# Moving three things in a two-layer attention kernel on one core: the load of the norms' factors, one weight block, and the splitting of the next layer's memory

## The chip, the core and the metric

The kernel runs on one core of a Trainium2 chip. The engines are TensorE (PE: matrix products and transposes), ScalarE (ACT), VectorE (DVE) and GpSimd (POOL); SyncE (SP) only issues transfers. The metric is the time of one execution in device microseconds (us); the median of several runs is given, and one execution is also recorded by the hardware profiler.

## The reference

Two layers transform `x` (256 x 1024) with a memory `mem` (256 x 1024). In each layer 16 heads of 64 attend: six over a causal block, six in a dilated pattern, four over the memory. Everything is float32.

```python
def hybrid_layer(x, mem, norm_g, w_in, w_out, mem_norm_g, w_mem_kv, qk_g):
    h = rms_norm(x, norm_g)
    proj = jnp.einsum('btd,de->bte', h, w_in)
    ...
    a_q, a_k, a_v, a_g, b_q, b_k, b_v, b_g, m_q, m_g = jnp.split(proj, cuts, axis=-1)
    qa = rope(rms_norm(to_heads(a_q, N_HEADS_MOBA), qk_g[0]))
    ...
    oa = from_heads(moba_attention(qa, ka, to_heads(a_v, N_HEADS_MOBA)))
    ...
    ob = from_heads(dilated_attention(qb, kb, to_heads(b_v, N_HEADS_DIL)))
    mkv = jnp.einsum('bmd,de->bme', rms_norm(mem, mem_norm_g), w_mem_kv)
    m_k, m_v = jnp.split(mkv, 2, axis=-1)
    ...
    om = from_heads(memory_attention(qm, km, to_heads(m_v, N_HEADS_MEM)))
    y = jnp.concatenate([oa * jax.nn.silu(a_g), ob * jax.nn.silu(b_g), om * jax.nn.silu(m_g)], axis=-1)
    return x + jnp.einsum('bte,ed->btd', y, w_out)

def reference(x, mem, norm_g, w_in, w_out, mem_norm_g, w_mem_kv, qk_g):
    for layer in range(DEPTH):
        x = hybrid_layer(x, mem, norm_g[layer], w_in[layer], w_out[layer],
                         mem_norm_g[layer], w_mem_kv[layer], qk_g[layer])
    return x
```

With 256 rows the causal heads have a single block, so they attend causally within it; the three dilated patterns become one mask with logarithms of counts.

## The kernel before

**Split products.** A float32 product is made of three faster ones: each operand is split into a rounded part and a rest. Of a weight tile (`raw`) ACT makes `hi` with a cast (L430) and DVE the rest `lo` (L431). Of the activations, transposed so that the 1024 inner elements lie in eight blocks of 128 partitions, ACT makes `xmh`, scaled by the norm's factors (L183), and DVE `xml` (L186), both in `split_x`, two blocks at a time. PE runs hi·xmh, hi·xml and lo·xmh into `acc` (L111). PE also transposes by a product with `ident` (L114).

**The factors.** `gT` (128 x 32, 16 KB) holds the factors of both layers' norms of `x` and of `mem`, one column to a block. It is loaded at the start from POOL (L85), whose transfers go by a software queue. The memory of each layer is `memT`, the transposed memory, times its columns of `gT`; in layer 0 the first two blocks are not split but scaled whole (`whole`, L494), and multiplied with `raw` in full float32.

**Loads.** `load_mem` (L99) loads pieces of `memT` through SP; `loads` (L409) issues the weights unit by unit. The first unit (`raw0`, four blocks of 256 KB of the first layer's `w_mem_kv`) goes through ACT's queue, everything after through SP's, in the order of the code at L450 to L465. The weights of w_in follow as buffers (three) come free.

**Order of the work.** PE's instructions are kept in the order of the code (`pe`). Beside that, generators are spawned with a delay on a modelled clock; `poll` runs those that are due at each step of a projection. So `pair_of_heads` and `head` (scores `wk`<-`qkT`, the negated maximum `nm` L332, exponentials `pr` L334, their scaling L347, the transposes of `pr`, the copy `pT` L358, the products `o`) are woven between the projections of the next heads. `next_mem` is such a generator, too: it splits the next layer's memory, two blocks (two `xmh`, two `xml`) each time it is resumed, four times, with D_NEXT_MEM of the model's clock between.

**A layer** projects memory keys and values, `mq`, `mg`; then for kind 2 (the dilated side, the second one in the weights: `bq`, `bk`, `bv`, `bg`) and then kind 0 (the causal side, the first one: `aq` to `ag`) it runs `project`, `normed`, `start_heads`, `gates`; then the output products. `normed` needs the head's sums of squares `hss` (L263), `ms`, a power on POOL (`hrs`, L156), and tables `tab` of rotation times factors that POOL builds after the memory's heads are started (L204 to L209: four `tab` operations for each of the kinds 0 to 3, in this order, and one scaling ahead of kind 0 and of kind 2). `t` (L267) is the first instruction to read the part of the table of kind 2. What runs between two kinds is set by `poll`, and the order on ACT, DVE and POOL is then laid down by a scheduler where `pin` doesn't hold it.

Of the kernel before, what the change touches and what calls it, by code (L numbers as in the profile page):

```python
# [22 lines left out]
DEPTH = 2  # L23
# [43 lines left out]
def hybrid_kernel(ctx: ExitStack, tc: tile.TileContext, x, mem, mem_t, gains, w_in, w_out, w_mem_kv, qk_g, const, out):  # L67
    nc = tc.nc
# [13 lines left out]
    mhalf = cp.tile([P, 16], F32, name="mhalf")  # L82
    nc.vector.memset(mhalf, -0.5)
    gT = cp.tile([P, 32], F32, name="gT")
    tc.keep_in_program_order(nc.gpsimd.dma_start(gT, gains))  # L85
    ident = cp.tile([P, P], F32, name="ident")
    make_identity(nc, ident)
    pinning = [True]
# [1 line left out]
    def pin(ins):  # L90

        return tc.keep_in_program_order(ins) if pinning[0] else ins
# [5 lines left out]
    def load_mem(k0, k1):  # L98
        pin(nc.sync.dma_start(memT[:, k0:k1], mem_t[k0 * P:k1 * P, :].rearrange("(k p) t -> p k t", p=P)))  # L99
# [34 lines left out]
    def spawn(gen, delay):  # L134
        tasks.append([clock[0] + delay, gen])
# [30 lines left out]
    def xm_tiles():  # L166
        return [sp.tile([P, KD, T], F32R, tag=c, name=c, bufs=2) for c in ("xmh", "xml")]
# [48 lines left out]
    def project(xs, chunk, n):  # L216

        accs = [acc_p.tile([P, 512], F32, tag="acc", name="acc")[:, :n] for _ in range(NT)]

        def steps():  # L220
            for k0, nk, w in chunk:
                if len(w) == 1:
                    for k in range(nk):
                        for t in range(NT):
                            mm(accs[t], whole[k0 + k][:, t * P:(t + 1) * P], w[0][:, k], start=k0 + k == 0, stop=False)
                        yield
                    continue
                for ks in [range(nk)] if pinning[0] and nk < 4 else [[k] for k in range(nk)]:
                    products([(accs[t], k0 + k, [x[:, k0 + k, t * P:(t + 1) * P] for x in xs], [p[:, k] for p in w])
                              for t in range(NT) for k in ks], 0, KD - 1)  # L230
                    yield

        return accs, steps()

    def project_t(xs, chunk, n):

        accs = [acc_p.tile([P, 512], F32, tag="acc", name="acc")[:, :T] for _ in range(n // P)]

        def steps():
            for k0, nk, w in chunk:  # L240
                for k in range(nk):
                    products([(acc, k0 + k, [x[:, k0 + k] for x in xs], [p[:, k, e * P:(e + 1) * P] for p in w])
                              for e, acc in enumerate(accs)], 0, KD - 1, x_moves=True)
                    yield

        return accs, steps()

    def run(projection):
        accs, steps = projection
        for _ in steps:  # L250
            poll()
        return accs
# [4 lines left out]
    def normed(acc, n, dst, tables):  # L257

        h = n // HD
        sq = sp.tile([P, n], F32, tag="sq", name="sq", bufs=2)  # L260
        pin(nc.scalar.activation(sq, acc, AF.Square))
        ss = sp.tile([P, h], F32, tag="hss", name="hss", bufs=4)
        pin(nc.vector.tensor_reduce(ss, heads(sq), axis=AX.X, op=ALU.add))  # L263
        rs = sp.tile([P, h], F32, tag="hrs", name="hrs", bufs=4)
        rsqrt(rs, ss, h, 1.0 / HD)
        t1 = sp.tile([P, n], F32, tag="t1", name="t1", bufs=2)
        pin(nc.vector.tensor_tensor(heads(t1), heads(acc), tables[0][:, None, :].to_broadcast([P, h, HD]),  # L267
                                    op=ALU.mult))
        if len(tables) > 1:
            t2 = sq  # L270
            half = dict(s=2, d=HD // 2)
            pin(nc.vector.tensor_tensor(t2.rearrange("p (h s d) -> p h s d", **half),
                                        acc.rearrange("p (h s d) -> p h s d", **half)[:, :, ::-1, :],
                                        tables[1].rearrange("p (s d) -> p s d", s=2)[:, None]
                                        .to_broadcast([P, h, 2, HD // 2]), op=ALU.mult))
            pin(nc.vector.tensor_tensor(t1, t1, t2, op=ALU.add))
        pin(nc.vector.tensor_tensor(heads(dst), heads(t1), rs.unsqueeze(2).to_broadcast([P, h, HD]), op=ALU.mult))
# [111 lines left out]
    def loads():  # L389
        while loaded[0] < len(units):  # L390
            u = loaded[0]
            loaded[0] += 1
            i, a, nk, n = units[u]
            l, c = order[i]
            if c == "mkv":
                src = w_mem_kv[l]
            elif c in in_cols:
                src = w_in[l][:, in_cols[c][0]:in_cols[c][0] + n]
            else:
                src = w_out[l][e_rows[c][0] * P:, :]  # L400
            if u == 0:
                raws[u] = sp.tile([P, nk, n], F32, tag="yT0", name="raw0", bufs=1)
            else:
                raws[u] = wp.tile([P, nk, n], F32, tag="raw", name="raw", bufs=RAW_BUFS)
            step = 1 if u == 0 else 2 if u == 1 else 4 if u == 2 else nk
            for b in range(0, nk, step):
                e = b + step
                queue = nc.scalar if u == 0 else nc.sync
                pin(queue.dma_start(raws[u][:, b:e],  # L409
                                    src[(a + b) * P:(a + e) * P, :].rearrange("(k p) n -> p k n", p=P)))  # L410
                yield
# [24 lines left out]
    def weights():  # L436

        i = at[0]
        at[0] += 1
        while at[1] < len(splits) and units[splits[at[1]][0]][0] == i:  # L440
            s = at[1]
            at[1] += 1
            split(s + ahead[0])
            yield splits[s][1], splits[s][2], parts[s]
# [5 lines left out]
    for k in range(4):  # L450
        next(loading)
        if k < 2:
            load_mem(k, k + 1)
        elif k == 2:
            load_mem(2, 4)
    pin(nc.scalar.activation(cp.tile([P, 16], F32, name="table"), mhalf, AF.Square))
    load_mem(4, 6)
    next(loading)
# [13 lines left out]
    def next_mem(dst, g):  # L472

        for k2 in range(0, KD, 2):
            pinning[0] = True
            split_x(dst, memT[:, k2:k2 + 2], g, k2)
            pinning[0] = False
            yield D_NEXT_MEM

    for l in range(DEPTH):  # L480
# [47 lines left out]
        def gates(accs, dst):  # L528
            for e, acc in enumerate(accs):
                th = sp.tile([P, T], F32, tag="th", name="th", bufs=2)  # L530
                nc.scalar.activation(th, acc, AF.Tanh, scale=0.5)
                nc.vector.scalar_tensor_tensor(dst[:, e], th, 1.0, acc, op0=ALU.add, op1=ALU.mult)

        def head_tiles(n, nv):
            return [sp.tile([P, NT, n], F32, tag=c, name=c, bufs=1) for c in ("qn", "kn")] + [
                sp.tile([P, NT, nv], F32, tag="v", name="v", bufs=2),
                sp.tile([P, n // P, T], F32, tag="gate", name="gate", bufs=2)]
# [8 lines left out]
        def start_heads(pairs, e0, qn, kn, masks, v, gate, ready, delay=D_NORM):  # L546
            for pair in range(pairs):
                spawn(pair_of_heads(qn, kn, pair, masks, v, gate, ready,
                                    lambda y, e=e0 + pair: finished(y, e)), delay + D_PAIR * pair)
# [30 lines left out]
        for kind, e0 in ((2, 3), (0, 0)):  # L580
            if kind == 2:
                masks = [cst[:, C_DIL:C_DIL + 128], cst[:, C_DIL + 128:C_DIL + 384]]
            else:
                masks = [cst[:, C_CAUSAL + 128:C_CAUSAL + 256], cst[:, C_CAUSAL:C_CAUSAL + 256]]
            if l + 1 < DEPTH and kind == 2:
                mem_xs = xm_tiles()
                spawn(next_mem(mem_xs, gT[:, 24 + 8 * l:32 + 8 * l]), D_FIRST_MEM)
            qn, kn, v, gate = head_tiles(384, 384)
            ready = dict(v=1e9, gate=1e9)
            for i, dst in ((0, qn), (1, kn)):  # L590
                for t, acc in enumerate(run(project(xs, weights(), 384))):
                    normed(acc, 384, dst[:, t], (tab[:, kind + i, 0, t], tab[:, kind + i, 1, t]))
            start_heads(3, e0, qn, kn, masks, v, gate, ready)
            for t, acc in enumerate(run(project(xs, weights(), 384))):
                nc.scalar.copy(v[:, t], acc)
            ready["v"] = clock[0] + D_EVAC
            gates(run(project_t(xs, weights(), 256)), gate[:, 0:2])
            gates(run(project_t(xs, weights(), 128)), gate[:, 2:3])
            ready["gate"] = clock[0] + D_EVAC
# [64 lines left out]
```

## Time and profile before

| what | value |
|---|---|
| runs, median (lowest to highest) | 296.41 us (295.67 to 296.65), 3 runs |
| profiled execution | 295.58 us |
| its span | 293.8 us |
| PE busy | 285.1 us, 97% |
| DVE busy | 204.5 us, 70% |
| ACT busy | 200.1 us, 68% |
| POOL busy | 56.0 us, 19% |
| HBM read | 45.96 MB, 160 GB/s over the span |

The span runs from the first to the last recorded instruction; the time of the execution is 1.8 us longer. An engine that is busy for a small share may still hold up PE for a moment; these moments are found in the waits and timelines, not in this table.

### The profile page before, as it was taken

How to read it: one execution, taken by the hardware profiler on the slowest of the kernel's cores; microseconds unless marked ns; L12 is line 12 of the kernel's file. 1: busy time of each engine (PE TensorE's matmuls, PEld its weight loads, DVE VectorE, ACT ScalarE, POOL GpSimd, SP SyncE). 2: the span in 40 equal slices, each digit the busy share in tenths (PEclk: the TensorE clock that was granted, in tenths of full speed). 3: DMA queues.
4: the chain of work that ended last, by engine and by line, in shares of the span. 5: the costliest groups of instructions: out<-in, count | busy, mean ns of one | idle time of the engine just before them, and what ended most of it. 6: DMA issues, size and time to landing. Idle time of an engine off the chain costs nothing.

```text
span 293.8 us, 4977 instructions
## 1 busy us (share of the span) xinstructions
PE 285.1 (97%) x1810; PEld 250.2 (85%) x1810; DVE 204.5 (70%) x456; ACT 200.1 (68%) x445; POOL 56.0 (19%) x74
## 2 busy tenths in 40 slices
PE   7799999999999999999999999999999999999994
PEld 5489989698998999877788999989899899987773
DVE  1588899887656997654485668879655699765413
ACT  2799968795888646987364654868588864698600
POOL 1003598030001230000011049703000123000000
PEclk9999999999999999999999999999999999999999
DMA  7999656327347248246207726560823715820003
GB/s 231 378 366 355 208 143 229 78 102 220 106 113 240 62 158 310 98 166 207 80 8 243 222 101 174 189 172 9 274 60 108 240 47 170 304 99 29 3 0 143
DMA packets 32681, 47.33 MB, mean 161 GB/s; under 512 B 1152, under 2 KB 27536, under 8 KB 32656
## 3 DMA queue, kind: packets, MB, share of 16 engines
q1 hardware_dynamic: 32048, 45.95, 48.4%
q10 hardware_dynamic: 576, 1.05, 1.0%
q8 instruction: 14, 0.23, 0.3%
q14 instruction: 11, 0.09, 0.1%
q0 software_dynamic: 32, 0.02, 0.0%
HBM read 45.96 MB, written 1.05 MB: 160 GB/s over the span
## 4 chain that ended last, share of the span: by engine, by line
PE 81%; DVE 6%; DMA 5%; ACT 3%; issue 2%; POOL 1%; SPq 0%; DVEq 0%; ACTq 0%
PE acc L111 64%; PE wk L114 7%; PE o L111 5%; PE wk L111 5%; DMA raw<-in_w_in_dram 3%; DMA memT<-in_mem_t_dram 2%; DVE lo L431 2%; DVE xml L186 1%; ACT hi L430 1%; POOL hrs L156 1%; DVE hss L263 1%; ACT xmh L183 1%; POOL r L156 0%; DVE ms L155 0%; ACT pr L334 0%
## 5 line engine op out<-in xcount | busy, mean ns | idle before, releaser
L431 DVE TENSOR_TENSOR lo<-raw,hi 128x768 fp32r<-128x768 f32 (+1 forms) x91 | 97.2, 1091 | 31.0 <-ACT hi L430 30.9
L430 ACT CAST hi<-raw 128x768 fp32r<-128x768 f32 (+1 forms) x91 | 83.8, 937 | 33.0 <-PE acc L111 24.4
L111 PE MATMUL acc<-hi,xmh 128*128 128x384 f32 (+2 forms) x252 | 67.0, 348 | 1.7 <-ACT hi L430 1.7
L111 PE MATMUL acc<-hi,xml 128*128 128x384 f32 (+2 forms) x252 | 63.6, 335 | 0.0
L111 PE MATMUL acc<-lo,xmh 128*128 128x384 f32 (+2 forms) x252 | 63.5, 335 | 0.0
L156 POOL TENSOR_TENSOR hrs<-ms,mhalf 128x6 f32<-128x6 f32 (+1 forms) x24 | 30.3, 1264 | 118.9 <-DVE ms L155 118.5
L111 PEld LDWEIGHTS acc<-hi,xmh 128*128 128x128 f32 x252 | 42.6, 189 | 7.1 <-issue 3.0
L111 PEld LDWEIGHTS acc<-lo,xmh 128*128 128x128 f32 x252 | 45.0, 188 | 1.2
L111 PEld LDWEIGHTS acc<-hi,xml 128*128 128x128 f32 x252 | 44.9, 188 | 1.2
L111 PE MATMUL acc<-hi,yT 128*128 128x512 f32 x128 | 41.0, 402 | 0.0
L111 PE MATMUL acc<-xmh,hi 128*128 128x256 f32 x128 | 29.7, 293 | 0.0
L341 ACT ACTIVATE pr<-pr,nm 128x128 f32<-128x128 f32 (+1 forms) x48 | 21.4, 446 | 12.0 <-DVE nm L339 11.8
L111 PE MATMUL acc<-xmh,lo 128*128 128x256 f32 x128 | 28.4, 283 | 0.0
L111 PE MATMUL acc<-xml,hi 128*128 128x256 f32 x128 | 28.3, 282 | 0.0
L111 PEld LDWEIGHTS acc<-hi,yT 128*128 128x128 f32 x128 | 23.0, 188 | 4.9 <-issue 0.7
L347 ACT ACTIVATE pr<-pr,rinv 128x128 f32<-128x128 f32 (+1 forms) x64 | 25.6, 462 | 0.0
L111 PE MATMUL acc<-lo,yT 128*128 128x512 f32 x64 | 25.0, 391 | 0.0
L111 PEld LDWEIGHTS acc<-xmh,hi 128*128 128x128 f32 x128 | 20.9, 191 | 0.7 <-issue 0.7
L111 PEld LDWEIGHTS acc<-xml,hi 128*128 128x128 f32 x128 | 21.0, 191 | 0.0
L111 PEld LDWEIGHTS acc<-xmh,lo 128*128 128x128 f32 x128 | 21.0, 191 | 0.0
L358 ACT COPY pT<-wk 128x384 f32<-128x384 f32 (+1 forms) x32 | 15.5, 506 | 6.8 <-PE wk L114 6.8
L339 DVE CUSTOM_DVE_ANT_0 pr<-wk,cst 128x128 f32<-128x128 f32 (+1 forms) x48 | 14.3, 354 | 5.3 <-PE wk L111 5.3
(77 smaller groups left out, 356.8 us busy)
## 6 DMA issues: line engine op xcount, KB each, us to landing
raw<-in_w_in_dram SPq DMA_DIRECT2D x24, 768.0 KB, 4.9
raw<-in_w_in_dram SPq DMA_DIRECT2D x7, 1024.0 KB, 5.3
raw<-in_w_out_dram SPq DMA_DIRECT2D x6, 1024.0 KB, 6.1
raw<-in_w_in_dram SPq DMA_DIRECT2D x6, 512.0 KB, 3.7
raw<-in_w_out_dram SPq DMA_DIRECT2D x4, 512.0 KB, 4.3
raw<-in_w_mem_kv_dram SPq DMA_DIRECT2D x2, 1024.0 KB, 5.2
raw<-in_w_mem_kv_dram ACTq DMA_DIRECT2D x4, 256.0 KB, 5.4
raw<-in_w_mem_kv_dram SPq DMA_DIRECT2D x2, 512.0 KB, 7.5
```

The lines of the kernel that those rows point to most:

```text
L111: pe(nc.tensor.matmul(out, a, b, start=start, stop=stop), us)
L114: pe(nc.tensor.transpose(out, a, ident), 0.109)
L156: pin(nc.gpsimd.tensor_tensor(dst, ms, mhalf[:, :n], op=ALU.pow))
L183: pin(nc.scalar.activation(hi[:, k], v[:, a], AF.Copy, scale=g[:, k:k + 1]))
L186: pin(nc.vector.scalar_tensor_tensor(lo[:, k], v[:, a], g[:, k:k + 1], hi[:, k].bitcast(F32), op0=ALU.mult, op1=ALU.subtract))
L263: pin(nc.vector.tensor_reduce(ss, heads(sq), axis=AX.X, op=ALU.add))
L339: nc.vector.tensor_tensor_reduce(out=pr[:, spans[t]], in0=s[:, spans[t]], in1=masks[t], scale=-1.0, scalar=3e38, op0=ALU.add, op1=ALU.min, ...
L341: nc.scalar.activation(pr[:, spans[t]], pr[:, spans[t]], AF.Exp, scale=-1.0, bias=nm[:, t:t + 1], accum_out=sums[:, t:t + 1])
L347: nc.scalar.activation(pr[:, spans[t]], pr[:, spans[t]], AF.Copy, scale=rinv[:, t:t + 1])
L358: nc.scalar.copy(pT[:, :n], ps[:, :n])
L430: pin(nc.scalar.copy(hi, raw))
L431: pin(nc.vector.tensor_tensor(lo, raw, hi.bitcast(F32), op=ALU.subtract))
```

## The change

Three edits. The load of `gT` leaves POOL and is issued by SP, second in its queue, behind the first block of `memT`. The fourth block of the first weight unit leaves ACT's queue and is issued by SP, fifth in its queue. And `next_mem` is spawned at the start of kind 0 (the first side's projections), where it was spawned at the start of kind 2 (the second side's). Only layer 0 has a next layer.

```diff
--- before.py
+++ after.py
@@ -82,7 +82,6 @@
     mhalf = cp.tile([P, 16], F32, name="mhalf")
     nc.vector.memset(mhalf, -0.5)
     gT = cp.tile([P, 32], F32, name="gT")
-    tc.keep_in_program_order(nc.gpsimd.dma_start(gT, gains))
     ident = cp.tile([P, P], F32, name="ident")
     make_identity(nc, ident)
     pinning = [True]
@@ -405,7 +404,7 @@
             step = 1 if u == 0 else 2 if u == 1 else 4 if u == 2 else nk
             for b in range(0, nk, step):
                 e = b + step
-                queue = nc.scalar if u == 0 else nc.sync
+                queue = nc.scalar if u == 0 and b < 3 else nc.sync
                 pin(queue.dma_start(raws[u][:, b:e],
                                     src[(a + b) * P:(a + e) * P, :].rearrange("(k p) n -> p k n", p=P)))
                 yield
@@ -453,6 +452,8 @@
             load_mem(k, k + 1)
         elif k == 2:
             load_mem(2, 4)
+        if k == 0:
+            pin(nc.sync.dma_start(gT, gains))
     pin(nc.scalar.activation(cp.tile([P, 16], F32, name="table"), mhalf, AF.Square))
     load_mem(4, 6)
     next(loading)
@@ -582,7 +583,7 @@
                 masks = [cst[:, C_DIL:C_DIL + 128], cst[:, C_DIL + 128:C_DIL + 384]]
             else:
                 masks = [cst[:, C_CAUSAL + 128:C_CAUSAL + 256], cst[:, C_CAUSAL:C_CAUSAL + 256]]
-            if l + 1 < DEPTH and kind == 2:
+            if l + 1 < DEPTH and kind == 0:
                 mem_xs = xm_tiles()
                 spawn(next_mem(mem_xs, gT[:, 24 + 8 * l:32 + 8 * l]), D_FIRST_MEM)
             qn, kn, v, gate = head_tiles(384, 384)
```

The first rows are of SP's queue, from the program's start: each is a transfer, `memT` the transposed memory, `raw` weights.

```order
L99 DMA memT<-in_mem_t_dram 128x256 x2
L99 DMA memT<-in_mem_t_dram 128x2x256 x2
L409 DMA raw<-in_w_mem_kv_dram 128x2x512
L448 DMA x_sb<-in_x_dram 128x1024 x2
L99 DMA memT<-in_mem_t_dram 128x2x256
```

The same place in the changed kernel; `raw_96` is the fourth block of the first weight unit.

```order
L98 DMA memT<-in_mem_t_dram 128x256
L456 DMA gT<-in_gains_dram 128x32
L98 DMA memT<-in_mem_t_dram 128x256
L98 DMA memT<-in_mem_t_dram 128x2x256
L408 DMA raw_96<-in_w_mem_kv_dram 128x512
L98 DMA memT<-in_mem_t_dram 128x2x256
L408 DMA raw<-in_w_mem_kv_dram 128x2x512
L447 DMA x_sb<-in_x_dram 128x1024 x2
```

`gT` stands between the first two blocks of `memT`, and the weight block between its two larger pieces; what follows is one and two places further back.

The next rows are of DVE, from the last `kn` of the memory's heads to the first normed products of kind 2, in the kernel before; `nm` is the maximum that the first memory heads' softmax starts with.

```order
L277 TENSOR_TENSOR kn<-t_386,hrs 128x256
L186 SCALAR_TENSOR_TENSOR xml<-memT,gT,xmh 128x256 x2
L431 TENSOR_TENSOR lo<-raw,hi 128x768 x2
L186 SCALAR_TENSOR_TENSOR xml<-memT,gT,xmh 128x256 x2
L431 TENSOR_TENSOR lo<-raw,hi 128x768 x3
L332 TENSOR_REDUCE nm<-wk 128x2 x2
L263 TENSOR_REDUCE hss<-sq 128x6
L345 RECIPROCAL rinv<-sums 128x2
L267 TENSOR_TENSOR t_610<-acc,tab 128x384
```

The same place in the changed kernel; `t_596` is the product with POOL's table that stood further back before.

```order
L276 TENSOR_TENSOR kn<-t_386,hrs 128x256
L430 TENSOR_TENSOR lo<-raw,hi 128x768 x4
L262 TENSOR_REDUCE hss<-sq 128x6
L266 TENSOR_TENSOR t_596<-acc,tab 128x384
L154 TENSOR_SCALAR ms<-hss 128x6
L331 TENSOR_REDUCE nm<-wk 128x2 x2
L271 TENSOR_TENSOR sq<-acc,tab 128x384
L344 RECIPROCAL rinv<-sums 128x2
```

The four `xml` are gone, a `lo` moved behind, and `nm` now follows `hss`, `t_596` and `ms`, where it preceded `hss` and `t_610`.

The last rows are of ACT, where the causal heads of layer 0 run between the projections of kind 0, before.

```order
L358 COPY pT<-wk 128x384
L347 ACTIVATE pr<-pr,rinv 128x128
L347 ACTIVATE pr<-pr,rinv 128x256
L430 CAST hi<-raw 128x768 x3
L543 CAST yT_254<-y 128x256
L358 COPY pT<-wk 128x384 x2
```

The same place in the changed kernel.

```order
L357 COPY pT<-wk 128x384
L346 ACTIVATE pr<-pr,rinv 128x128
L346 ACTIVATE pr<-pr,rinv 128x256
L182 ACTIVATE xmh<-memT,gT 128x256 x2
L429 CAST hi<-raw 128x768
L182 ACTIVATE xmh<-memT,gT 128x256 x2
L429 CAST hi<-raw 128x768 x2
L544 CAST yT_254<-y 128x256
L357 COPY pT<-wk 128x384 x2
```

Two pairs of `xmh` stand among the three casts, ahead of `yT` and the two `pT`.

## Rows read from the trace of the kernel before

**Rows 1.** Windows: PE, PEld, DVE, ACT, POOL busy, granted clock, DMA share, GB/s.

```profile
0.00:20.00 20.00, 16.08 (x70) 12.20 (x71) 9.37 (x20) 11.46 (x20) 2.59 (x9) 1.00 0.94 318
```

**Rows 2.** Waits of PE: operation and releaser: us, times, longest.

```profile
PE acc L111 <- ACT hi L430: 1.7, 1, 1.7
PE acc L111 <- DVE whole L494: 1.2, 1, 1.2
```

**Rows 3.** Timeline of PE, layer 0: start, us, instruction, [idle before <-releaser].

```profile
38.73 0.33 PE L114 MATMUL wk<-ident,kn 128*128 128x128 f32 x1 [0.46 <-DVE kn L277]
...
49.99 1.03 PE L114 MATMUL wk<-ident,pr 128*128 128x128 f32 x8
...
53.19 1.13 PE L111 MATMUL wk<-qkT 64*128 64x256 f32 x6 [0.48 <-ACT pT L358]
...
55.49 1.08 PE L111 MATMUL o<-pT,v 128*64 128x256 f32 x8
```

**Rows 4.** Timeline of PE, layer 1, the same place of the program.

```profile
190.98 1.04 PE L114 MATMUL wk<-ident,pr 128*128 128x128 f32 x8
...
193.02 1.13 PE L111 MATMUL wk<-qkT 64*128 64x256 f32 x8
...
195.34 1.08 PE L111 MATMUL o<-pT,v 128*64 128x256 f32 x8
```

**Rows 5.** Timeline of the opening.

```profile
5.15 0.62 DVE L494 TENSOR_SCALAR whole<-memT,gT 128x256 f32<-128x256 f32 x2 [4.13 <-DMA gT<-in_gains_dram]
...
9.04 0.91 ACT L183 ACTIVATE xmh<-memT,gT 128x256 fp32r<-128x256 f32 x2 [4.89 <-DMA memT<-in_mem_t_dram]
```

**Rows 6.** Timeline of ACT, layer 0.

```profile
27.26 0.83 ACT L430 CAST hi<-raw 128x768 fp32r<-128x768 f32 x1 [0.58 <-DMA raw<-in_w_in_dram]
...
50.29 0.91 ACT L183 ACTIVATE xmh<-memT,gT 128x256 fp32r<-128x256 f32 x2
51.09 1.56 ACT L430 CAST hi<-raw 128x768 fp32r<-128x768 f32 x2
52.55 1.07 ACT L358 COPY pT<-wk 128x512 f32<-128x512 f32 x2
```

**Rows 7.** Chain that ended last: start, us, what.

```profile
19.07 8.12 DMA raw<-in_w_in_dram
```

**Rows 8.** Timeline of DVE, layer 0.

```profile
38.60 1.09 DVE L186 SCALAR_TENSOR_TENSOR xml<-memT,gT,xmh 128x256 fp32r<-128x256 f32 x2
39.61 2.08 DVE L431 TENSOR_TENSOR lo<-raw,hi 128x768 fp32r<-128x768 f32 x2
...
45.44 1.27 DVE L332 TENSOR_REDUCE nm<-wk 128x2 f32<-128x512 f32 x2
...
47.28 0.54 DVE L267 TENSOR_TENSOR t<-acc,tab 128x384 f32<-128x384 f32 x1
```

**Rows 9.** Timeline of POOL, layer 0.

```profile
40.84 1.03 POOL L207 TENSOR_TENSOR tab<-gB,cst 128x64 f32<-128x64 f32 x1
...
44.91 0.78 POOL L207 TENSOR_TENSOR tab<-gB,cst 128x64 f32<-128x64 f32 x1
...
45.95 0.31 POOL L207 TENSOR_TENSOR tab<-gB,cst 128x64 f32<-128x64 f32 x1
```

**Rows 10.** Timeline of ACT, the first side.

```profile
84.55 1.56 ACT L430 CAST hi<-raw 128x768 fp32r<-128x768 f32 x2
86.75 0.83 ACT L430 CAST hi<-raw 128x768 fp32r<-128x768 f32 x1 [0.64 <-PE acc L111]
...
87.91 0.85 ACT L358 COPY pT<-wk 128x384 f32<-128x384 f32 x2
```

**Rows 11.** Timeline of PE, the first side.

```profile
88.69 0.93 PE L111 MATMUL wk<-qkT 64*128 64x128 f32 x8
...
101.45 0.51 PE L111 MATMUL acc<-lo,xmh 128*128 128x384 f32 x2
```

**Rows 12.** Timeline of DVE, the first side.

```profile
97.79 0.95 DVE L431 TENSOR_TENSOR lo<-raw,hi 128x768 fp32r<-128x768 f32 x1
```

## The prediction

> **What bounds the kernel now.** I read the table of engines first. TensorE (PE) is busy for 97% of the span, with the granted clock at 1.00 in the opening [rows 1] and at nine tenths or more in every slice of the page, so no edit to ScalarE (ACT), VectorE (DVE), GpSimd (POOL) or a queue counts unless it lets PE start something sooner or makes it wait. The view of PE's waits comes next. Its two large ones are at the opening [rows 2]: 1.2 us for `whole`, the first scaled memory blocks, and 1.7 us for the first `hi`. The timelines show two waits of about half a microsecond each later on [rows 3]: 0.46 at 38.73 for `kn`, and 0.48 at 53.19 for the copy `pT`. I then laid layer 1 over layer 0, since they run the same PE program [rows 3, 4]. From the transposes of `pr` to the first `o` layer 0 takes 55.49 − 49.99 = 5.50 us, layer 1 takes 195.34 − 190.98 = 4.36. The difference of 1.14 us is what layer 0 loses there. After 55 us PE has no gap of this kind in layer 0.
>
> **Edits 1 and 2, the opening.** `whole` waits 4.13 us for gT and starts at 5.15 [rows 5]. Second in SyncE's queue, gT can land sooner; I put it at 1 us, somewhere inside those 4.13, so that PE's first products start 1 us sooner. The sum does not hang on this figure. The gain has to pass two further stops. The first is the `hi` of the wait of 1.7: it stands behind `xmh` at 9.04, which waited 4.89 us for a block of memT [rows 5], not for gT. So PE would only wait longer there, save for the few tenths by which memT can land earlier because 256 KB leave ACT's queue, or later because SyncE's queue is two transfers longer. The second stop is at 38.73, where PE waits for `kn` [rows 3]. `kn` is the end of a serial chain of DVE, POOL and ACT that begins with the cast at 27.26, which ACT reached 0.58 us too early: it waited for weights [rows 6]. That transfer was issued at 19.07 and took 8.12 us [rows 7], with the DMA engines busy 0.94 of the first 20 us at 318 GB/s [rows 1]: it is bound by the bytes ahead of it, and edits 1 and 2 move the same bytes. An earlier arrival is therefore swallowed at 27.26, and a later one of up to 0.58 us too. I cost the opening at 0. The bounds from the rows are −0.58 (all of ACT's idle time, if the weights too land that much sooner) and +0.6 (as much, if they land that much later).
>
> The Trainium skill, page "DMA: Bandwidth & Descriptors", section "Latency and other measured facts", gives as a best guess for slower DMA engines 7 and 15 the descriptor rings of the software queue, which POOL's load uses and which the change leaves empty. By that guess the early weights could land sooner; no row here shows it, and it is the rule behind rival B below.
>
> **Edit 3, what it takes away.** In layer 0's second gap the `pT` copy starts at 52.55 on ACT because it stands behind two `xmh` (50.29, 0.80 until the next instruction) and two casts (51.09, 1.46) [rows 6]. Those `xmh` go, so this copy can start 0.80 sooner, which is a sure part. PE's wait is 0.48 at 53.19, and six of the eight scores stand behind it [rows 3]; in layer 1 they stand together at 193.02, 2.04 after the transposes [rows 4]. To have no gap, `pT` must be there at 49.99 + 2.04 = 52.03, and for the second head some 0.2 later.
>
> DVE's part decides the rest. Before, DVE did two `xml`, two `lo`, two `xml`, three `lo`, then `nm` at 45.44 and `t` at 47.28 [rows 8]. Now it does four `lo`, then `hss`, `t`, `ms`, and `nm` only behind them. `nm` is no longer behind the memory's splits, but behind `t`, which reads the table that POOL is building; behind `nm` stand ACT's exponentials, `pr`, and PE's transposes. Its time: four `lo` from 38.60 at 2.08 / 2 = about 1.0 each end at 42.6, `hss` takes about as long as `t`, 0.54, so DVE is free for `t` at 43.1 to 43.5 (`hss` may itself wait for ACT's squares). POOL must do ten operations for the part of the table that `t` reads (eight of the first two kinds, one scaling, one of the third kind). POOL's operations take 1.03 when they lie beside DVE's `lo`, and 0.31 when they do not [rows 9]. About one is done per `lo`, so four by 42.6, and the last six at 0.31 take 1.9: the table is ready at 44.5. `t` takes 0.54, so `nm` starts at about 45.1, against 45.44: 0.3 sooner.
>
> From `nm` to the end of the `pr` before the `xmh` is 50.29 − 45.44 = 4.85 us before, which I keep [rows 6, 8]. So `pr` is done at 49.9, the two casts at 51.4, and the first `pT`, at 1.07 / 2 plus its hand-over, some 0.64, at 52.0. PE wants it at 52.03. The gap then closes: I take the whole 1.14. The bounds: with `nm` at its old time the gain is 0.8, the `xmh` alone; with the table only ready when its part was ready before, at 44.91 + 0.78 = 45.69 [rows 9], `nm` starts at 46.3, 0.85 later, and the 0.8 are given back: gain 0.
>
> The Trainium skill, page "SBUF — State Buffer", section "Who interferes with whom", says that a VectorE instruction with two SBUF inputs and a GpSimd instruction that reads SBUF lock each other out. The 1.03 beside a `lo` and 0.31 without agree with it, and it speaks against this change: four `lo` in a row lie on the table, and by the rule alone the six operations would be no faster if DVE kept reading two SBUF inputs; here DVE turns to a reduction and a wait instead.
>
> **Edit 3, what it adds.** The eight `xmh` (0.40 each) and eight `xml` now fall among the first side's projections, where PE had no gap. The first four `xmh` enter ACT's queue between two `pr` and a cast, and between that cast and the next. ACT's row of before: casts from 84.55 (two, 1.46), idle for 0.64, a cast at 86.75, `yT`, and `pT` from 87.91 [rows 10]. After: 0.81 (two `xmh`) + 0.72 (cast) + 0.81 + 0.72 + 0.72 + 0.31 (`yT`) from 84.55 is 88.64, the idle time of 0.64 and some hand-overs being used up. So `pT` is 0.73 late: the first of the two copies, 0.85 / 2 and a hand-over of 0.06, ended at 88.39 and ends at 89.12 now. The scores at 88.69 need it after the first two of eight, 0.93 × 2/8 = 0.23 later, at 88.92 [rows 11]. So PE waits 0.20, and with another hand-over 0.26. If none of the 1.62 were hidden, the cost would be 1.62 less the slack of 0.53, that is 1.09; if ACT's waits swallow them all, 0. The other four `xmh` and the `xml` fall at about 94 to 100 us. The tightest there is a `lo` that ended at about 98.7 [rows 12] and is needed at 101.45 [rows 11]: 2.7 of slack, against four `xml` at 1.09 a pair [rows 8], 2.2, so 0.5 is left. I take no stall; if ACT's 0.81 for a pair of `xmh` comes on top, its price is 0.3.
>
> **Sum.** −1.14 + 0.26 + 0 = −0.88. The profiled execution of 295.58 us becomes 294.70; it lay 0.83 below the median of the runs, 296.41, to which I apply the same difference: 295.53. 0.3% of the median, about what a measurement of this kernel can tell from no change, is 0.89 us.
>
> **Rivals.**
> *A, the forecast.* The gap closes mostly and the first side costs a little: 295.2 to 295.9, half of it past the 0.3%.
> *B, the opening pays as well.* gT and the weights land sooner, and the chain at 27.26 gains its 0.58: 295.53 − 0.58 = 294.95. For it: ACT really idles there for a DMA [rows 6]. Against: the wire is full [rows 1].
> *C, the gap moves instead of closing.* The change does not do what it says: `nm` waits behind `t` for the table until it is as late as before, the sure 0.8 is given back, and the first side's 0.26 is paid: 296.67. If 0.3 to 0.6 of the gain stay, 296.1 to 296.4. For it: the table's last operation is a wait that DVE did not have before, with a margin of only 0.3. Against: POOL runs at 0.31 as soon as DVE stops its `lo` [rows 9].
> *E, slower.* The same wait, longer: if four of POOL's last six operations take 1.03, as at 40.84, and not 0.31, the table is ready at 44.5 + 4 × 0.72 = 47.3, `nm` at 47.9, 2.5 later than before: +2.5 − 0.8 + 0.26 = +1.9, 298.3. It decides when the table comes later than about 46.3.
>
> **How the numbers follow.** A 0.46, B 0.18, C 0.24, E 0.12. Faster: 0.18 + half of A = 0.41. Within 0.3%: the other half of A and C = 0.47. Slower 0.12. The time is A's, 295.5. The range takes in B at its middle with some 0.35 below it, and C to its end with 0.2 above: 294.6 to 296.9; E and the extremes of B and C, under 2 in 10, are left out.
>
> **What would show it.** `whole` and PE's first products about a microsecond sooner, with a longer wait before 11 (edits 1, 2). PE at 38.7 as now. On DVE, `t` directly after `hss`, waiting for POOL for one microsecond or so, and `nm` at about 45.1; on PE one block of eight scores at about 52 and `o` at 54.4. If `nm` is at 46 or later, C or E. At 88.9 a PE wait of 0.2 to 0.3 for `pT`, and none at 101. I am wrong if POOL's operations do not speed up after the `lo`, if PE waits on a moved split at 90 to 104, or if `kn` moves at 38.73.

## The result, and the profile after

In the first comparison the changed kernel took 294.31 us in the median of 6 runs (294.07 to 294.81), the kernel before 296.35 (295.50 to 297.03, 6 runs): a ratio of 0.9936, interval 0.9916 to 0.9956. In a later comparison, on chip 2, it was 294.40 against 295.54 (29 runs of before), 0.9959, interval 0.9945 to 0.9972. The changed kernel's time hardly differs between the two; that of the kernel before does. The forecast was 295.5, which is 1.2 us above the changed kernel's median in the first comparison.

The profiled execution took 294.36 us (span 292.6), 1.22 less than that of before, where the forecast had 0.88. First, PE's timeline in layer 0 after the change; the rows answer to [rows 3].

```profile
38.55 0.33 PE L113 MATMUL wk<-ident,kn 128*128 128x128 f32 x1 [0.95 <-DVE kn L276]
...
49.86 1.03 PE L113 MATMUL wk<-ident,pr 128*128 128x128 f32 x8
...
51.88 1.20 PE L110 MATMUL wk<-qkT 64*128 64x256 f32 x8
...
54.25 1.08 PE L110 MATMUL o<-pT,v 128*64 128x256 f32 x8
```

From the transposes of `pr` to `o` it is 54.25 − 49.86 = 4.39 us, where it was 5.50 and is 4.36 in layer 1: the gap closed, by 1.11 of the 1.14 forecast. The eight scores stand together, and the 0.48 for `pT` is gone. The wait for `kn` grew from 0.46 to 0.95, and stands 0.18 earlier. DVE's timeline (answers to [rows 8]):

```profile
38.42 3.94 DVE L430 TENSOR_TENSOR lo<-raw,hi 128x768 fp32r<-128x768 f32 x4
42.89 0.55 DVE L262 TENSOR_REDUCE hss<-sq 128x6 f32<-128x384 f32 x1 [0.53 <-ACT sq L260]
44.43 0.56 DVE L266 TENSOR_TENSOR t<-acc,tab 128x384 f32<-128x384 f32 x1 [0.99 <-POOL tab L206]
44.91 0.16 DVE L154 TENSOR_SCALAR ms<-hss 128x6 f32<-128x6 f32 x1
44.98 1.28 DVE L331 TENSOR_REDUCE nm<-wk 128x2 f32<-128x512 f32 x2
```

`t` waits for POOL 0.99 us, and `nm` starts at 44.98, forecast 45.1. POOL's timeline ([rows 9]) shows why the wait ended there:

```profile
41.51 1.03 POOL L208 TENSOR_TENSOR tab<-gB,cst 128x64 f32<-128x64 f32 x1
42.51 0.32 POOL L206 TENSOR_TENSOR tab<-gB,cst 128x64 f32<-128x64 f32 x1
...
44.08 0.32 POOL L206 TENSOR_TENSOR tab<-gB,cst 128x64 f32<-128x64 f32 x1
```

Four operations of 1.03 to 1.10 lie under the four `lo`; after the end of the last `lo` they take 0.32, and the part of the table that `t` needs is there at 44.40 (forecast 44.5). ACT's timeline of the second gap ([rows 6]):

```profile
49.03 0.92 ACT L346 ACTIVATE pr<-pr,rinv 128x256 f32<-128x256 f32 x2
49.84 1.57 ACT L429 CAST hi<-raw 128x768 fp32r<-128x768 f32 x2
51.30 1.07 ACT L357 COPY pT<-wk 128x512 f32<-128x512 f32 x2
```

No `xmh` stands between `pr` and the casts any more. In the first side, where the splits went, ACT's timeline ([rows 10]) is

```profile
82.99 0.89 ACT L182 ACTIVATE xmh<-memT,gT 128x256 fp32r<-128x256 f32 x2
83.79 0.82 ACT L429 CAST hi<-raw 128x768 fp32r<-128x768 f32 x1
84.52 0.91 ACT L182 ACTIVATE xmh<-memT,gT 128x256 fp32r<-128x256 f32 x2
85.33 1.55 ACT L429 CAST hi<-raw 128x768 fp32r<-128x768 f32 x2
...
87.09 0.84 ACT L357 COPY pT<-wk 128x384 f32<-128x384 f32 x2
```

and PE's row that answers to the scores of [rows 11]

```profile
87.45 1.08 PE L110 MATMUL wk<-qkT 64*128 64x128 f32 x8
```

With the 1.24 by which `o` is earlier taken off, `pT` would have started at 86.67 as before, so it is 0.42 late, not 0.73; the scores took 1.08 and not 0.93, and cost 0.15. At the opening the factors' wait, PE's first products and the waits of ACT read (timelines of DVE, PE and ACT, [rows 5, 6]):

```profile
4.34 0.35 DVE L495 TENSOR_SCALAR whole<-memT,gT 128x256 f32<-128x256 f32 x1 [3.34 <-DMA gT<-in_gains_dram]
```

```profile
4.75 4.61 PE L110 MATMUL acc<-raw,whole 128*128 128x512 f32 x8 [0.36 <-DVE whole L495]
...
9.27 1.21 PE L110 MATMUL acc<-hi,xmh 128*128 128x512 f32 x4
```

```profile
7.37 0.91 ACT L182 ACTIVATE xmh<-memT,gT 128x256 fp32r<-128x256 f32 x2 [3.74 <-DMA memT<-in_mem_t_dram]
...
27.09 0.83 ACT L429 CAST hi<-raw 128x768 fp32r<-128x768 f32 x1 [2.10 <-DMA raw<-in_w_in_dram]
```

PE's first products start 0.80 us sooner (4.75 for 5.55), but the eight take 4.61 us instead of 3.70 and so end no sooner. The opening ran 1.7 us ahead at `xmh` (7.37 for 9.04), because the block of `memT` landed that much sooner (7.28 for 8.95), and PE's wait of 1.7 for the first `hi` is gone (9.27 for 10.97). At the cast of the first bq weights, the first weights of the dilated side's queries, 0.17 of it was left: ACT waits 2.10 there instead of 0.58.

### The profile page after: what moved, and what is told of

Read it like the earlier page. It is cut to its first block, busy times and chain, and to the rows that moved or that the text cites. A ratio compares the mean times of both kernels' runs of the same rounds, so it can differ in the third digit from the quotient of the medians.

```text
span 292.6 us, 4974 instructions
## 1 busy us (share of the span) xinstructions
PE 285.8 (98%) x1810; PEld 250.6 (86%) x1810; DVE 204.3 (70%) x456; ACT 200.0 (68%) x445; POOL 53.8 (18%) x73
## 4 chain that ended last, share of the span: by engine, by line
PE 86%; DMA 7%; DVE 3%; POOL 1%; issue 1%; ACT 1%; SPq 0%; DVEq 0%; ACTq 0%
PE acc L110 68%; PE wk L113 7%; PE wk L110 5%; PE o L110 5%; DMA raw<-in_w_in_dram 3%; DMA x_sb<-in_x_dram 2%; DVE lo L430 1%; DMA raw<-in_w_mem_kv_dram 1%; POOL hrs L155 1%; DVE hss L262 0%; ACT xn L160 0%; POOL r L155 0%; DVE ms L154 0%; DVE kn L276 0%; ACT hi L429 0%
```

## The experiments

Each was compared with runs of the kernel before on its chip. Four kernels did the parts of the change.

**The splitting alone** (edit 3): 294.46 against 295.47, ratio 0.9962 (0.9943 to 0.9981).

> The splitting moved, both loads as before. Theory G (the gain is the closed gap, the opening is swallowed at the wait for weights): 1.9 us faster than before like the whole change, o at about 54.3 in the profile. Theory O (the gap gives 1.1 to 1.2, and the loads give the other 0.8 in the usual execution): 1.2 us faster.

**Both loads alone** (edits 1 and 2): 294.84, ratio 0.9976 (0.9964 to 0.9987).

> Both loads moved, the splitting as before. Theory G: within 0.3 us of the kernel before, PE's first products about a microsecond sooner and the wait for kn longer by as much. Theory O: 0.8 us faster, with the weights for the cast at 27.26 landing sooner in the usual execution.

**The factors' load alone** (edit 1): 296.45, ratio 1.0024 (1.0004 to 1.0044): about 0.7 us slower by the ratio.

> Only the factors' load moved from POOL's software queue to SyncE's. Theory G: no change within 0.3 us. Theory O: 0.8 us faster, all of the loads' part, because no transfer of the software queue is left to hold up two of the sixteen engines; the memory's second pair lands at about 7 and not at 8.95.

**The fourth block alone** (edit 2): 294.81, ratio 0.9972 (0.9959 to 0.9985).

> Only the fourth weight block moved to SyncE's queue, the factors still by POOL. Both theories: no change within 0.3 us; the late landings of the memory's second pair (8.95 before) stay.

By the ratios the splitting gives 1.1 us and the two loads 0.7, near the sizes of theory O; theory G's forecast for the loads, no change, did not come. But the loads' gain comes with the weight block and not, as O had it, with the factors: the block alone gives 0.8, and with the block moved no difference shows whether the factors move too (294.84 and 294.81). The factors' move alone loses. Its profile shows a delay in ACT's issues and in its first cast of a split block:

```profile
0.72 3.88 ACTq L408 DMA_DIRECT2D raw<-in_w_mem_kv_dram  x4
...
10.58 1.04 ACT L429 CAST hi<-raw 128x1024 fp32r<-128x1024 f32 x1 [2.54 <-DMA raw<-in_w_mem_kv_dram]
```

ACT's four issues take until 4.60 (before they took 1.88 us in all): the fourth starts only at 4.26, as the first transfer has landed at 4.24, because the factors' load is now one more transfer ahead of it. With the block in SyncE's queue as well, ACT's three issues take 1.37 and the later one waits in SyncE's. But that delay does not explain the loss: the execution shown took 295.02 us and a second profiled one, with the fourth issue at 3.96 and that cast at 10.02, 294.44; both are less than the 295.47 of the kernel before. The record of the runs shows something else. In nine of the twelve runs the mean granted clock of TensorE was 0.994 or 0.988, and they took 296.18 to 297.96; in the other three it was 0.998 to 1.000, and they took 294.90 to 295.74. Of the 83 runs of the kernel before that stand beside these experiments four had 0.994, at 295.30 to 295.68, and no run of another kernel was under 0.997. So the loss lies in the runs at the lower mean clock; none of these was profiled, and why it was lower, and whether that costs the time, is open.

**More executions of the same kernels.** I profiled the kernel before three times more, and the changed kernel and its parts once more.

> The kernel before, profiled again, to see what differs between its executions, 294.7 to 297.3 apart. Theory S: where it is slow, some engines land the opening's transfers over 1 us after the others. Theory W: where it is slow, the weights for the cast at 27.26 land later, whatever the opening did.

> As the look before it, a third profile of the kernel before.

> A fourth profile of the kernel before. Theory Q (four weight blocks in ACT's queue leave some of the sixteen engines about 2 us behind the median one, up to the weights for bq): 1.5 to 2 us behind at the third load of layer 0's w_in, weights at 27.2 or later. Theory N (the lag comes by chance, whatever the queues): anything from 0.3 to 2.

> A second profile of the splitting moved alone, whose opening is that of the kernel before; its first profile had a lag of 0.55 only. Theory Q: 1.5 to 2 us in this one. Theory N: anything from 0.3 to 2. By both, kn to o takes 15.7.

> A second profile of the fourth block moved alone. Theory Q: a lag under 0.6, weights at about 26.8. Theory N: anything from 0.3 to 2. By both, kn to o takes 16.3.

> A third profile of the changed kernel. Theory Q: a lag under 0.6, weights at 26.7 to 27.0. Theory N: anything from 0.3 to 2. By both, kn to o takes 15.7.

> A second profile of the factors' load moved alone, 0.7 us slower by its runs though its first profile lay 1.4 below its median. If the late opening costs it (the fourth weight block is issued only when the first has landed, PE's first split products at 11.7 and not at 11.0): the wait for kn ends at 39.5 to 40.5, by the same 11.5 behind the cast of the first bq weights, and kn to o takes 16.3.

With all profiles together the time falls into pieces, all from timelines: the start of the cast of the first bq weights on ACT; PE's last `kn` transpose of the first pair; the first `nm` on DVE; the first `o` on PE; the end. From `o` to the end of the execution it is 239.9 to 240.3 us in all twenty profiles. So nearly all that differs lies ahead of `o`. Fifteen of the twenty:

| profile | time | cast | cast to `kn` | `kn` to `nm` | `nm` to `o` |
|---|---|---|---|---|---|
| before | 295.58 | 27.26 | 11.47 | 6.71 | 10.05 |
| before, 2nd | 296.75 | 27.58 | 11.47 | 7.58 | 10.06 |
| before, 3rd | 297.71 | 28.80 | 11.47 | 7.25 | 10.06 |
| before, 4th | 296.53 | 28.23 | 11.47 | 6.70 | 10.09 |
| splitting alone | 295.10 | 27.79 | 11.46 | 6.12 | 9.53 |
| splitting alone, 2nd | 295.80 | 27.68 | 11.61 | 7.05 | 9.27 |
| loads alone | 294.98 | 27.27 | 11.46 | 6.25 | 10.06 |
| factors alone | 295.02 | 27.20 | 11.61 | 6.18 | 10.08 |
| factors alone, 2nd | 294.44 | 26.67 | 11.60 | 6.16 | 10.06 |
| block alone | 294.75 | 26.90 | 11.48 | 6.25 | 10.07 |
| block alone, 2nd | 294.66 | 26.74 | 11.60 | 6.19 | 10.07 |
| changed | 294.36 | 27.09 | 11.46 | 6.43 | 9.27 |
| changed, 2nd | 294.11 | 26.84 | 11.45 | 6.42 | 9.29 |
| changed, 3rd | 294.81 | 27.57 | 11.46 | 6.41 | 9.27 |
| changed, half of the memory later (below) | 293.78 | 25.57 | 12.29 | 6.12 | 9.53 |

Three things are read from it. **`nm` to `o`**: 10.06 without the moved splitting, 9.27 with it wherever `nm` was not early anyway: 0.79, the two `xmh` of 0.80. **`kn` to `nm`**: 6.7 to 7.6 before, 6.1 to 6.4 in every kernel with a moved load. DVE's timeline of the second profile of before, and ACT's cast that its `lo` waits for:

```profile
42.87 2.06 DVE L431 TENSOR_TENSOR lo<-raw,hi 128x768 fp32r<-128x768 f32 x2
45.75 0.96 DVE L431 TENSOR_TENSOR lo<-raw,hi 128x768 fp32r<-128x768 f32 x1 [0.82 <-ACT hi L430]
46.63 1.28 DVE L332 TENSOR_REDUCE nm<-wk 128x2 f32<-128x512 f32 x2
```

```profile
44.88 0.84 ACT L430 CAST hi<-raw 128x768 fp32r<-128x768 f32 x1 [2.86 <-DMA raw<-in_w_in_dram]
```

`nm` stands behind a third `lo`, whose cast waits for weights from memory: 1.25 us in the profiled execution of before (at 42.95), 2.86 here. In the kernels with the factors or the block moved the scheduler puts that `lo` behind `nm`; only where half of the memory is moved behind the weights too (below) does it stand ahead again. The same stretch of DVE, the block alone:

```profile
42.17 2.07 DVE L431 TENSOR_TENSOR lo<-raw,hi 128x768 fp32r<-128x768 f32 x2
44.17 0.54 DVE L263 TENSOR_REDUCE hss<-sq 128x6 f32<-128x384 f32 x1
44.63 1.27 DVE L332 TENSOR_REDUCE nm<-wk 128x2 f32<-128x512 f32 x2
...
49.60 0.95 DVE L431 TENSOR_TENSOR lo<-raw,hi 128x768 fp32r<-128x768 f32 x1
```

The splitting alone keeps the `lo` ahead of `nm`. In its first profile the `lo` waits 1.43 and `nm` still comes 6.12 behind `kn`; in the second it waits 2.43, and `nm` comes 7.05 behind:

```profile
39.07 3.94 DVE L431 TENSOR_TENSOR lo<-raw,hi 128x768 fp32r<-128x768 f32 x4
45.44 0.98 DVE L431 TENSOR_TENSOR lo<-raw,hi 128x768 fp32r<-128x768 f32 x1 [2.43 <-ACT hi L430]
46.34 1.27 DVE L332 TENSOR_REDUCE nm<-wk 128x2 f32<-128x512 f32 x2
```

The gains of the two parts overlap between `kn` and `o`: 16.8 to 17.6 us before, 16.2 to 16.3 with loads moved, 15.7 and 16.3 with the splitting moved, 15.7 with both. So 1.1 and 0.7 need not add up, and the whole change was not run on the chip of the parts.

**Cast to `kn`** is 11.45 to 11.48 wherever that cast waited for its weights, whatever PE did before, but for the kernel of the next experiment: the chain that the prediction named. Where the weights were there first (both profiles of the factors alone, the second ones of the block and of the splitting) it is 11.60, and the cast stands behind ACT's own earlier work. The cast itself lies at 27.26 to 28.80 before (four profiles, mean 27.97) and at 26.84 to 27.57 after (three, mean 27.17). The three later executions of before, at 296.53 to 297.71, were slower than the usual one: the medians of the runs on their chips were 295.68 and 295.56. So 0.8 is more than these means can show of the usual execution.

**The wait for the weights.** The changed kernel with half of the untransposed memory (512 KB) behind the bq weights:

```diff
-    pin(nc.sync.dma_start(mem_sb, mem.rearrange("(t p) c -> p t c", p=P)))
+    pin(nc.sync.dma_start(mem_sb[:, 0], mem[0:P]))
...
+            if i == 1 and l == 0:
+                pin(nc.sync.dma_start(mem_sb[:, 1], mem[P:2 * P]))
```

> The changed kernel with the second half of the untransposed memory loaded behind the first bq weights, which the earlier trial did not bring about (there it was still issued ahead of them). Theory W (their landing swallows the opening): they land at about 25.5 and not at 27.02, the cast at 27.09 comes 1.4 us sooner, and the kernel is 0.6 to 1.6 us faster than the changed one. Rival V (PE's own chain sets the wait for kn): no change within 0.3 us against it.

```profile
37.86 0.33 PE L113 MATMUL wk<-ident,kn 128*128 128x128 f32 x1 [0.95 <-DVE kn L276]
```

The cast came at 25.57 (26.84 in the changed kernel beside it), nearly as theory W has it, but `kn` only 0.43 sooner, at 37.86, 12.29 behind the cast. DVE's timeline shows where the other 0.8 went, first here and then in the changed kernel:

```profile
27.32 0.41 DVE L262 TENSOR_REDUCE hss<-sq 128x4 f32<-128x256 f32 x1
27.72 0.96 DVE L430 TENSOR_TENSOR lo<-raw,hi 128x768 fp32r<-128x768 f32 x1
28.59 0.17 DVE L154 TENSOR_SCALAR ms<-hss 128x4 f32<-128x4 f32 x1
```

```profile
28.84 0.41 DVE L262 TENSOR_REDUCE hss<-sq 128x4 f32<-128x256 f32 x1
29.28 0.17 DVE L154 TENSOR_SCALAR ms<-hss 128x4 f32<-128x4 f32 x1
```

The scheduler put another `lo` between `hss` and `ms`, which belong to the chain; from the cast to `ms` it is 3.02 us where it was 2.19, and from `ms` to `kn` 9.27 in both. So the edit did two things: the earlier weights do move `kn`, and a new order takes two thirds of it back. The time was 294.25 against 294.40 (ratios 0.9961 and 0.9959), the same within their intervals, with a wider spread (293.24 to 295.65). Theory W's 0.6 to 1.6 us did not come and the time is as rival V has it, but not by V's reason. A second profile (294.00 us, cast 25.79, `kn` 38.08) agrees with the first.

> A second profile of the kernel with half of the untransposed memory behind the first bq weights, whose runs spread from 293.2 to 295.7. If the engines that lag set its slow runs: a lag of 1 us or more here in a run above 294.5 and weights at 26.5 or later; if not, weights at 25.5 again and the time near 293.8.

An earlier attempt put the second half right behind the first gains:

> The changed kernel with the second half of the untransposed memory (512 KB, 1.5 us of the wire) loaded behind the first bq weights instead of ahead of them. Theory W (the wait for these weights, 2.10 us of idle ACT at 27.09, is what swallows the opening): the weights land at about 25.5 and not at 27.02, PE's waits of 0.77 at 32.01 and 0.95 at 38.55 shrink or vanish, and the kernel is 1.0 to 1.6 us faster than the changed one, 293. Rival V (PE's own chain sets 38.55, the weights only look late): no change within 0.3 us against the changed kernel.

There it was still issued ahead of the weights, so nothing was tested; 294.98, ratio 0.9976 (0.9957 to 0.9996).

**The software queue.** The changed kernel with a load of the same 16 KB by POOL into a tile that nothing reads:

```diff
+    spare = cp.tile([P, 32], F32, name="spare")
+    tc.keep_in_program_order(nc.gpsimd.dma_start(spare, gains))
```

> The changed kernel with an added load of the same 16 KB by POOL's software queue at the start into a tile that nothing reads. Theory S (the software queue's load holds up two of the sixteen engines): 0.4 to 0.8 us slower than the changed kernel, executions more than 1 us apart, landings of the first ten transfers in two groups. Theory R (only the order in the queues counts, which transfer is the ninth and waits for the first to land): within 0.3 us of the changed kernel.

294.12 against 295.68, ratio 0.9939 (0.9914 to 0.9963), no slower than the changed kernel's 0.9936 and 0.9959: theory S falls.

**The queues.** All four blocks in SyncE's queue (`queue = nc.sync`):

> The changed kernel with all four blocks of the first weight unit in SyncE's queue, none in ACT's. Theory L (two queues that feed the same sixteen engines at the opening leave some engines behind, and these stay behind up to the weights for bq): the slowest engine is under 0.5 us behind the median one at 20 us, executions lie within 0.6 us of each other, and the time is that of the changed kernel or 0.3 us less. Rival I (what counts is how soon the transfers are issued): PE's first products start 0.3 to 0.5 us later and the time is 0 to 0.5 us more.

295.25, ratio 0.9986 (0.9974 to 0.9997), 0.85 us over the changed kernel; the profile has a cast at 28.79 and DMA engines 1.6 us behind. Theory L falls; rival I has the direction, with 0 to 0.5 for 0.85.

**Block and splitting without the factors:**

> The fourth weight block and the splitting moved, the factors still loaded by POOL. If the factors' move gives nothing (alone it made the kernel 0.7 us slower, with the block moved too it took nothing from the block's 0.8): 0.993 to 0.994 of the kernel before, as the whole change. If it takes back a part of the block's gain: 0.992 or less.

294.63, ratio 0.9971 (0.9959 to 0.9983), 0.23 us over the changed kernel with intervals that overlap: what the factors' move gives once the block has moved is not clear from it (the two kernels without the moved splitting, 294.84 and 294.81, show nothing).

**The changed kernel again**, beside these: 0.9959, not the 0.993 to 0.994 that I expected.

> The changed kernel once more, to stand beside the next three on one chip: 0.993 to 0.994 of the kernel before.

## Why the prediction was wrong in its size

- **The gap (−1.14).** Right, in both terms: 0.78 in the pair of profiles for the `xmh` (0.80), and `nm` 0.28 sooner behind `kn` (0.3), 1.06 together. The step on DVE and POOL came as worked out, `t` waiting 0.99 and all.
- **The first side (+0.26).** Too large. From `o` to the end it is 240.03 on average in the nine profiles without the moved splits and 240.19 in the eleven with them: 0.16. ACT reached the splits 0.3 us sooner than I had it. The 101.45 `lo` made no stall.
- **The opening (0).** The mechanism was right for the two kernels, the cast of the bq weights swallows the opening, and in the pair of profiles it gave 0.17. (In four of the twenty profiles, of parts of the change, that cast did not wait, and so would not have swallowed it.) The sentence that `memT` could land only a few tenths sooner was not: `xmh` came 1.67 sooner and PE's wait for `hi` went; the cast swallowed that, too. I had kept up to 0.58 for rival B, by a rule on the software queue that the spare load does not bear out.
- **The step that failed** is the last of the sum: "it lay 0.83 below the median of the runs, 296.41, to which I apply the same difference". The forecast of 295.53 lies 1.22 above the 294.31 measured. Of this 0.34 belongs to the terms: from profile to profile the sum has −0.88, and the change gave −1.22. The other 0.88 belongs to this step: the kernel before's profiled execution lay 0.83 below its median, that of the changed kernel (294.36) 0.05 above. I took what stood between one execution and the median as the same before and after. What the runs show in its place are two waits of the kernel before whose lengths change from execution to execution: that of the third `lo` ahead of `nm`, which stands in the rows of order in "The change", made `nm` come up to 0.87 later behind `kn` than in the first profile, and the bq weights' cast came 0.3 to 1.5 later. I had costed that `lo` as work of fixed length, which it was in the first profile, where DVE did not wait for it. The change takes it from its place, and in all three profiles of the changed kernel `nm` lies 6.41 to 6.43 behind `kn`. Whether it also shortens the weights' wait in the usual execution is not settled.
- **What is not shown** is that these waits made up the 0.83 in the first comparison: only one execution of the kernel before was profiled there. In the later comparisons, on three chips, the medians of the kernel before were 295.47 to 295.68, so that the first profile would have been a usual execution there; the change gave 1.14 in the one with both kernels, less than from profile to profile, and 295.58 − 0.88 = 294.70 would have been 0.3 above the 294.40 measured. So how far this step missed depended on which runs the first median came from.
- **Rivals.** C and E did not come: POOL's operations did speed up after the `lo`. The rows agree with the Trainium skill, page "SBUF — State Buffer", section "Who interferes with whom", in the form that I used: 1.03 beside a `lo`, 0.32 beside a reduction or a waiting DVE. The guess of the Trainium skill, page "DMA: Bandwidth & Descriptors", section "Latency and other measured facts", is not supported here: adding a software load did not slow the kernel.

What stays open: what lowers the mean clock in most runs of the factors alone, and whether that is what costs them 1.6 us (in both its profiles the cast of the bq weights did not wait for them, so that a later opening would not be swallowed there; that is argued, not shown); and what decides how far some DMA engines lag (below).

## What to carry to other kernels

Before a profile's difference is put on a median, look for waits on memory in that one execution that stand ahead of the critical instruction in an in-order queue: their length changes from run to run, and an edit that moves the instruction ahead of them can gain more than the one profile shows. Read the changed order for what leaves the place in front of the critical instruction, too, not only for what enters it. And an edit to a load can change more than the load: here the scheduler laid the splits of the weights in another order around `nm` and `ms`. That order made 0.46 of the 0.60 us that the profile with the loads alone gained on the first one, and took back 0.8 of the 1.3 that the later memory gave at the cast. So compare the order on every engine before a gain or its absence is put down to the transfer, and price such edits together: here the factors' load alone lost 0.7 us by the ratio, the block alone gained 0.8, and the two together 0.7.

## What I had not expected of the hardware

The landing of the first bq weights in sixteen parts, one for each DMA engine, as the trace records them: in the profiled execution of before thirteen by 25.75 and three between 26.95 and 27.19; after the change fifteen by 25.79 and one at 27.02; with half of the memory behind them fifteen by 24.35 and one at 25.50. In each of these a fetch of instructions, one packet of 16 KB that takes 1.1 to 1.2 us, starts shortly before (24.76, 23.13, 23.30). In the second profile of the block alone the fetch starts at 24.82 and all sixteen parts are there by 25.77; there the late part is in the next load (28.95, fifteen by 27.90). That a part waits behind the fetch is argued from these times, not tried. In four profiles of before the slowest engine was 1.5 to 2.0 us behind the median one at the load before, too (in the first, two parts came at 25.00 and 25.25 and fourteen by 23.72), so that before not all of the late parts can be the fetch's doing; in the eight with both loads moved as in the change it was 0.3 to 1.0, in the five with one of the two 0.4 to 0.6, with the splitting alone 0.6 and 0.9, with all blocks in SyncE's queue 1.6. Theory Q, four blocks in ACT's queue, wanted 1.5 to 2 with the splitting alone, whose opening is that of the kernel before, and under 0.6 in the third profile of the changed kernel, where it was 0.8; so it falls by its own figures, and what sets the lag stays open.

The first products of `whole` lie 0.86 us apart or 0.43: the record of the granted clock starts, at its full level (2.4 GHz), at 4.96 in the profile of before and at 6.63 after, at 4.0 to 10.5 over all profiles. Ahead of that nothing is recorded, and the view of windows prints 1.00 there, as in [rows 1]. In an execution where it came at 9.49 the eight products took 5.29 us instead of 3.70, all of it ahead of the cast of the bq weights.
